# Two transformer blocks in split fp32: modulation summed on VectorE, early matmuls of ones, low halves on GpSimd

## The chip, the cores and the metric

The kernel runs on one core of a Trainium2 chip. The metric is device time in microseconds of one execution, from the first to the last instruction and what the launch adds around it; lower is better. The engines are TensorE (PE in the profile, with its weight loads as PEld), VectorE (DVE), ScalarE (ACT), GpSimd (POOL) and SyncE (SP), which issues the transfers.

## The reference, cut to what matters

Two blocks work on x of 1 x 512 tokens x 1024, all in fp32. The first runs twice (two layers):

```
h = rms_norm(x, g_pre_mix[l])
q, k, v, cb, cc, cx, ga, gb = split(h @ w_in[l])
y_attn = band_attention(rope(q), rope(k), v, sink) @ w_attn_proj[l]
y_conv = (cb * short_conv(cc * cx, conv_w[l])) @ w_conv_proj[l]
x = x + rms_norm((sigmoid(ga) * y_attn + sigmoid(gb) * y_conv) @ w_out[l], g_post_mix[l])
h = rms_norm(x, g_pre_ffn[l])
x = x + rms_norm((silu(h @ w_gate[l]) * (h @ w_up[l])) @ w_down[l], g_post_ffn[l])
```

The second block runs once. A vector c of 1024 numbers gives six vectors of 1024 that shift, scale and gate its two halves: mod = silu(c) @ ada_w + ada_b, with ada_w of 1024 x 6144. Its first half has four mixers of four heads each: stick-breaking, differential, forgetting and native sparse attention; the second half is a feed-forward part with a short convolution. Of stick-breaking attention the change touches the part that needs, for each query, running sums over keys:

```
z = q @ k.T * scale
log_beta = log_sigmoid(z)
log_keep = where(past, log_sigmoid(-z), 0)
tail = cumsum(log_keep, reverse=True) - log_keep
a = where(past, exp(log_beta + tail), 0)
o = a @ v
```

## The kernel before, in words

Activations stand with features on the partitions and the 512 tokens along the free axis. Each matmul operand is split into a high half and a low half in fp32r, and a product is three matmuls: high by high, low by high, high by low (`mm_kb`, L523 to L525, 0.227 us apart for 512 columns). `split` (L514 to L516) makes the halves of an activation: ACT casts the high half, DVE subtracts it from the source for the low one. Weights come in units of 128 x 1024: `Stream` (L255 to L268) has SP issue the transfer `raw`, ACT cast `wh` and DVE subtract `wl`, some units ahead of use. `mblock` makes one block of 128 output features by 24 matmuls. The tile scheduler of the framework sets the order on each engine from the order of the code and its own simulated times; transfers, tiles and PSUM banks come from pools, and each engine works through its own list in order.

Modulation: `ada_step` (L906 to L930) is called twice in each of 12 blocks of the gate and up products of both layers (L725 to L727 in `ffn1`), 48 units in all. A unit is 128 rows of ada_w by 1024 columns; its transfer is `adaraw` (L934). DVE multiplies it by the silu of c, one number per partition, and adds it to `adaacc` (L918 for the first of eight, L920 for the others). After eight units the sum over partitions is eight fp32 matmuls of one column against ones (L927, each two passes on PE), and DVE adds the bias from `cols` into `mod` (L930). `ada_start` forms the silu of c by small operations at the program's start.

Start: `setup` issues the first transfers; `ones`, 128 x 128, is written by DVE (L357). The first products on PE are those of `Head`, `hd`, as the halves `hh` and `hl` of x come from ACT (L447) and DVE (L448) and the weights from `Stream`.

Stick-breaking heads: `S` computes scores into three PSUM banks, forms `rz` (softplus) for each by ACT and DVE (L1462), has GpSimd zero what is not past on the diagonal (`affine_select`, L1443, two on the third bank) and splits it into `sbk` (L1466, so L515 and L516). `C`, some steps later, sums `sbk` over keys on PE (L1484). Between the heads, `pipeline` puts pieces of the next mixers' preparation. In the last mixer, `osplit` (L1331) splits six of the eight blocks of mixer output `o` into `op2h` and `op2l` as background pieces, the last two after it; GpSimd scales that mixer's probabilities `pp` (L1158).

Of the kernel before, what the change touches and what calls it, by code (L numbers as in the profile page):

```python
# [9 lines left out]
F32 = mybir.dt.float32  # L10
F32R = mybir.dt.float32r
AF = mybir.ActivationFunctionType
OP = mybir.AluOpType

P = 128
# [17 lines left out]
def col_layout():  # L33
    off, lay = 0, {}

    def add(name, n):
        nonlocal off
        lay[name] = (off, n)
        off += n

    for l in range(DEPTH):
        for n in ("g_pre_mix", "g_post_mix", "g_pre_ffn", "g_post_ffn"):
            add(f"{n}{l}", NB)
        add(f"conv_w{l}", 3 * NB)
        add(f"sink{l}", NH)
    for n, c in (("c", NB), ("ada_b", 48), ("nmg", NB), ("nfg", NB), ("fcw", 3 * NF), ("fcb", NF), ("dgq", 1),
                 ("dgk", 1), ("lam", P), ("subg", 1), ("fgq", 1), ("fgk", 1), ("fbf", 4), ("ngq", 1), ("ngk", 3),
                 ("pe", 32)):
        add(n, c)
    return lay, off  # L50
# [9 lines left out]
def fm_cols(v):  # L60
    v = np.asarray(v)
    return v.reshape(-1, P).T
# [20 lines left out]
def pack(inp):  # L83
# [43 lines left out]
    def setc(name, v):  # L127
        o, n = lay[name]
        cols[:, o:o + n] = v
# [6 lines left out]
    setc("c", fm_cols(inp["c_2"][0]))  # L136
# [39 lines left out]
    for i in range(2):  # L176
# [20 lines left out]
        "ada": np.asarray(inp["ada_w_2"])[0].reshape(NB, P, 6, U).transpose(2, 0, 1, 3).reshape(48, P, U),  # L197
# [82 lines left out]
class Kern:  # L280
# [33 lines left out]

    TAIL = 4
# [22 lines left out]
    def setup(self):  # L338
# [18 lines left out]
        nc.vector.memset(self.ones, 1.0)  # L357
        self.mhalf = self.cpool.tile([P, 4], F32, name="mhalf")
# [155 lines left out]
    def split(self, hi, lo, src):  # L514
        self.nc.scalar.copy(hi, src)  # L515
        self.nc.vector.tensor_sub(lo, src, hi.bitcast(F32))  # L516
# [378 lines left out]
    def ada_start(self):  # L895
        nc = self.nc
        self.ca = self.cpool.tile([P, NB], F32, name="ca")
        o, _ = self.lay["c"]
        c = self.cols[:, o:o + NB]
        self.sigmoid_small(self.ca, c, [P, NB])  # L900
        nc.vector.tensor_mul(self.ca, self.ca, c)
        self.mod = self.cpool.tile([P, 48], F32, name="mod")
        self.ada_i = 0
        self.ada_raw = None

    def ada_step(self):  # L906
        nc = self.nc
        i = self.ada_i
        if i >= 48:
            return  # L910
        self.ada_i += 1
        if i == 0:
            self.ada_load(0)
        t = self.ada_raw
        g, kb = divmod(i, NB)
        if kb == 0:
            self.ada_acc = self.blk("adaacc", [P, U], F32)
            nc.vector.tensor_scalar(self.ada_acc, t, self.ca[:, 0:1], None, op0=OP.mult)  # L918
        else:
            nc.vector.scalar_tensor_tensor(self.ada_acc, t, self.ca[:, kb:kb + 1], self.ada_acc, op0=OP.mult,  # L920
                                           op1=OP.add)
        if i + 1 < 48:
            self.ada_load(i + 1)
        if kb == NB - 1:
            ps = self.ps("ada")
            for m in range(NB):
                nc.tensor.matmul(ps[:, m:m + 1], self.ada_acc[:, m * P:(m + 1) * P], self.ones[:, 0:1], start=True,  # L927
                                 stop=True)
            o = self.lay["ada_b"][0] + g * NB
            nc.vector.tensor_add(self.mod[:, g * NB:(g + 1) * NB], ps[:, :NB], self.cols[:, o:o + NB])  # L930
# [261 lines left out]
    def block2(self, tail, pend):  # L1192
# [137 lines left out]
        def osplit(m):  # L1330
            self.split(op_.hi[m], op_.lo[m], o[m])  # L1331
# [101 lines left out]
    def sb_head(self, hd, Q, KH, KL, V, o):  # L1433
# [18 lines left out]
        def S():  # L1452
# [3 lines left out]
            for b in range(3):  # L1456
# [8 lines left out]
                self.split(t[:, 0, sl], t[:, 1, sl], rz[:, sl])  # L1465
# [316 lines left out]
```

## Time and profile before

| | |
|---|---|
| time, median of 3 runs | 2462.95 us (2461.41 to 2464.72) |
| profiled execution, its own time | 2465.88 us |
| its span | 2464.2 us |
| mean granted TensorE clock | 0.991 |
| busy: PE, DVE, ACT, POOL | 2407.3, 1324.1, 996.1, 399.2 us |
| chain that ended last, by engine | PE 90%, DVE 3%, ACT 3%, POOL 2% |

Busy time is the time in which an engine has an instruction under way; matmuls overlap, so the step from one start to the next is what one costs, not its duration. The chain is followed back from the last instruction to what released each one. Times in the profile count from the span's start.

### The profile page before, as it was taken

What the parts mean: (1) busy time and instruction counts of PE and PEld (TensorE: products, weight loads), DVE (VectorE), ACT (ScalarE), POOL (GpSimd) and SP (SyncE); (2) the same over time, 40 slices, a digit from 0 to 9 for tenths busy, and PEclk for the clock granted to TensorE, in tenths of its full rate; (3) what the DMA queues carried; (4) which work ended last, traced back from release to release, by engine and by line L of the source; (5) the groups of instructions that cost most, each with busy time, mean ns of one, the idle gap of its engine ahead of it and who ended that gap; (6) DMA issues with size and microseconds to landing.
All of it is one profiled execution on the core that took longest, in us unless ns stands there. A gap on an engine that the chain in (4) does not pass through costs nothing.

```text
span 2464.2 us, 32671 instructions
## 1 busy us (share of the span) xinstructions
PE 2407.3 (98%) x12680; PEld 2073.7 (84%) x12680; DVE 1324.1 (54%) x2324; ACT 996.1 (40%) x1808; POOL 399.2 (16%) x437
## 2 busy tenths in 40 slices
PE   8999999999999999999999999999898899999999
PEld 8888888888888898888888888888788878888888
DVE  6777544366533177775434655422667586644531
ACT  4555423442223245554224322322375575333420
POOL 3433001211110034230012111100021232000000
PEclk9999999999999999999999999999799999999999
DMA  4511523355423244223233553332221204233350
GB/s 159 149 61 64 165 94 103 103 196 200 149 85 121 80 144 126 69 83 99 94 98 129 181 195 137 99 107 74 91 88 53 83 22 146 78 103 103 105 171 24
DMA packets 90115, 272.77 MB, mean 111 GB/s; under 512 B 10175, under 2 KB 19007, under 8 KB 89960
## 3 DMA queue, kind: packets, MB, share of 16 engines
q1 hardware_dynamic: 89960, 270.68, 33.1%
q8 instruction: 100, 1.64, 0.3%
q14 instruction: 55, 0.45, 0.1%
HBM read 249.65 MB, written 15.22 MB: 107 GB/s over the span
## 4 chain that ended last, share of the span: by engine, by line
PE 90%; DVE 3%; ACT 3%; POOL 2%; issue 2%; DMA 0%; SPq 0%; POOLq 0%; ACTq 0%; DVEq 0%
PE ps L523 24%; PE ps L525 24%; PE ps L524 24%; PE hd L524 2%; PE hd L525 2%; PE hd L523 2%; PE o L840 2%; PE pt L815 1%; PE tm L1025 1%; PE tm L1026 1%; PE tm L1027 1%; POOL t L576 1%; POOL t L575 1%; ACT pp L378 1%; PE s L791 1%
## 5 line engine op out<-in xcount | busy, mean ns | idle before, releaser
L268 DVE TENSOR_TENSOR wl<-raw,wh 128x1024 fp32r<-128x1024 f32 x382 | 477.5, 1267 | 346.6 <-ACT wh L267 283.2
L267 ACT CAST wh<-raw 128x1024 fp32r<-128x1024 f32 x382 | 390.0, 1050 | 188.6 <-DMA raw<-in_w_dram 99.0
L525 PE MATMUL ps<-hh,wl 128*128 128x512 f32 x752 | 295.3, 393 | 0.9 <-DVE wl L268 0.8
L524 PE MATMUL ps<-hl,wh 128*128 128x512 f32 x752 | 294.9, 392 | 0.0
L523 PE MATMUL ps<-hh,wh 128*128 128x512 f32 x752 | 294.4, 392 | 0.0
L524 PE MATMUL ps<-hfl,wh 128*128 128x512 f32 x640 | 249.3, 390 | 0.0
L523 PE MATMUL ps<-hfh,wh 128*128 128x512 f32 x640 | 249.1, 390 | 0.0
L525 PE MATMUL ps<-hfh,wl 128*128 128x512 f32 x640 | 248.9, 389 | 0.0
L525 PEld LDWEIGHTS ps<-hh,wl 128*128 128x128 f32 x752 | 141.3, 188 | 29.1 <-DVE wl L268 2.1
L524 PEld LDWEIGHTS ps<-hl,wh 128*128 128x128 f32 x752 | 141.2, 188 | 27.2
L523 PEld LDWEIGHTS ps<-hh,wh 128*128 128x128 f32 x752 | 141.2, 188 | 27.1 <-ACT ot L844 0.2
L525 PE MATMUL ps<-hidh,wl 128*128 128x512 f32 (+1 forms) x396 | 145.1, 366 | 0.0
L523 PE MATMUL ps<-hidh,wh 128*128 128x512 f32 (+1 forms) x396 | 144.9, 366 | 0.0
L524 PE MATMUL ps<-hidl,wh 128*128 128x512 f32 (+1 forms) x396 | 144.7, 365 | 0.0
L378 ACT ACTIVATE pp<-pp,at_nm 128x256 f32<-128x256 f32 (+1 forms) x208 | 114.4, 553 | 68.2 <-DVE at_nm L797 60.0
L525 PEld LDWEIGHTS ps<-hfh,wl 128*128 128x128 f32 x640 | 120.1, 188 | 24.9
L524 PEld LDWEIGHTS ps<-hfl,wh 128*128 128x128 f32 x640 | 120.2, 188 | 24.7
L523 PEld LDWEIGHTS ps<-hfh,wh 128*128 128x128 f32 x640 | 120.0, 188 | 24.8
L720 POOL TENSOR_TENSOR gs<-gs,R 128x512 f32<-128x512 f32 x44 | 71.4, 1623 | 377.6 <-ACT gs L378 366.6
L524 PE MATMUL ps<-h3l,wh 128*128 128x512 f32 x320 | 124.5, 389 | 0.0
L525 PE MATMUL ps<-h3h,wl 128*128 128x512 f32 x320 | 124.5, 389 | 0.0
L523 PE MATMUL ps<-h3h,wh 128*128 128x512 f32 x320 | 124.3, 389 | 0.0
(461 smaller groups left out, 5200.3 us busy)
## 6 DMA issues: line engine op xcount, KB each, us to landing
raw<-in_w_dram SPq DMA_DIRECT2D x382, 512.0 KB, 3.7
adaraw<-in_ada_dram SPq DMA_DIRECT2D x48, 512.0 KB, 5.6
xd<-xh SPq DMA_DIRECT2D x24, 256.0 KB, 2.1
xh<-xd SPq DMA_DIRECT2D x24, 256.0 KB, 3.1
xh<-in_x_dram SPq DMA_DIRECT2D x16, 256.0 KB, 5.0
Q<-ql SPq DMA_DIRECT2D x32, 128.0 KB, 3.4
bias_d<-row_d SPq DMA_DIRECT2D x8, 320.0 KB, 7.5
KH<-kst SPq DMA_DIRECT2D x16, 128.0 KB, 3.9
```

The lines of the kernel that those rows point to most:

```text
L267: nc.scalar.copy(hi, raw)
L268: nc.vector.tensor_sub(lo, raw, hi.bitcast(F32))
L378: i = nc.scalar.activation(out, in_, func, **kw)
L523: nc.tensor.matmul(ps[:, t], w[0][:, sl], h.hi[kb][:, t], start=first, stop=False)
L524: nc.tensor.matmul(ps[:, t], w[0][:, sl], h.lo[kb][:, t], start=False, stop=False)
L525: nc.tensor.matmul(ps[:, t], w[1][:, sl], h.hi[kb][:, t], start=False, stop=last)
L575: nc.gpsimd.tensor_mul(t2, t2, S)
L576: nc.gpsimd.tensor_add(t1, t1, t2)
L720: nc.gpsimd.tensor_mul(g, g, self.R)
L791: nc.tensor.matmul(ps[:, :n], q, KL[g][:, LO[i]:HI[i]], start=False, stop=True)
L815: nc.tensor.transpose(bank[:, c0:c0 + P], pslice(h, i)[:, c:c + P], self.ident)
L840: nc.tensor.matmul(ps[:, c0:c1], V[j][:, g * P:(g + 1) * P], t[b][:, a, c0:c1], start=(a == 0 and j == 0), stop=(a == 1 and j == 2))
```

## The change

The modulation's weights are handed over transposed: a unit is now 128 of the 6144 outputs on the partitions by the 1024 inputs. c comes as one row, broadcast by a transfer to all 128 partitions into `ca`, and ACT takes its silu, once for the units of each layer. Each unit is then one DVE instruction that multiplies it by `ca` in place, sums along the row and adds the bias into one column of `mod`; the matmuls of one column, the accumulator and the additions of the bias are gone, and so are the small operations of `ada_start` and the column c of `cols`. Units are loaded ahead within a layer, not from the first layer to the second. In `setup` eleven matmuls of ones by ones, 128 x 128, follow the writing of ones; they take one PSUM tile. `split` can be given another engine for the subtraction, which is GpSimd for `sbk` (12 subtractions) and for the six blocks of `osplit` in the last mixer.

```diff
--- before.py
+++ after.py
@@ -43,7 +43,7 @@
             add(f"{n}{l}", NB)
         add(f"conv_w{l}", 3 * NB)
         add(f"sink{l}", NH)
-    for n, c in (("c", NB), ("ada_b", 48), ("nmg", NB), ("nfg", NB), ("fcw", 3 * NF), ("fcb", NF), ("dgq", 1),
+    for n, c in (("ada_b", 48), ("nmg", NB), ("nfg", NB), ("fcw", 3 * NF), ("fcb", NF), ("dgq", 1),
                  ("dgk", 1), ("lam", P), ("subg", 1), ("fgq", 1), ("fgk", 1), ("fbf", 4), ("ngq", 1), ("ngk", 3),
                  ("pe", 32)):
         add(n, c)
@@ -133,7 +133,6 @@
             setc(f"{n}{l}", fm_cols(inp[n][l]))
         setc(f"conv_w{l}", fm_cols(inp["conv_w"][l]))
         setc(f"sink{l}", np.tile(inp["attn_sink"][l][None, :], (P, 1)))
-    setc("c", fm_cols(inp["c_2"][0]))
     setc("ada_b", fm_cols(inp["ada_b_2"][0]))
     setc("nmg", fm_cols(inp["norm_mix_g_2"][0]))
     setc("nfg", fm_cols(inp["norm_ffn_g_2"][0]))
@@ -194,7 +193,8 @@
         "onehot": onehot,
         "tab": np.ascontiguousarray(tab, np.float32),
         "phi": phib.reshape(P, 32 * P),
-        "ada": np.asarray(inp["ada_w_2"])[0].reshape(NB, P, 6, U).transpose(2, 0, 1, 3).reshape(48, P, U),
+        "ada": np.ascontiguousarray(np.asarray(inp["ada_w_2"])[0].T.reshape(48, P, U)),
+        "crow": np.ascontiguousarray(np.asarray(inp["c_2"])[0].reshape(1, U)),
         "x": np.ascontiguousarray(np.asarray(inp["x"])[0].T.reshape(NB, P, T).transpose(1, 0, 2).reshape(P, NB * T)),
     }
 
@@ -312,6 +312,7 @@
     def small(self, name, shape, dt=F32, bufs=3):
         return self.smp.tile(shape, dt, name=self.n(name), tag=name, bufs=bufs)
 
+    WARM = 11
     TAIL = 4
     NHF = 4
     NH3 = 4
@@ -355,6 +356,9 @@
         self.valid = self.cst[:, 512:520]
         self.ones = self.cpool.tile([P, P], F32, name="ones")
         nc.vector.memset(self.ones, 1.0)
+        ps = self.ps("pw")
+        for i in range(self.WARM):
+            nc.tensor.matmul(ps[:, :P], self.ones, self.ones, start=True, stop=True)
         self.mhalf = self.cpool.tile([P, 4], F32, name="mhalf")
         nc.vector.memset(self.mhalf, -0.5)
         self.R = self.cpool.tile([P, T], F32, name="R")
@@ -511,9 +515,9 @@
         rs[i] = self.rstd(acc2, HV[i])
         self.nc.scalar.copy(self.R[:, t0:t1], self.bcast(rs[i], 2)[:, :256])
 
-    def split(self, hi, lo, src):
+    def split(self, hi, lo, src, eng=None):
         self.nc.scalar.copy(hi, src)
-        self.nc.vector.tensor_sub(lo, src, hi.bitcast(F32))
+        (eng or self.nc.vector).tensor_sub(lo, src, hi.bitcast(F32))
 
     def mm_kb(self, ps, w, h, kb, first, last, wk=None, hv=(0, T)):
         nc = self.nc
@@ -893,41 +897,25 @@
         return F
 
     def ada_start(self):
-        nc = self.nc
-        self.ca = self.cpool.tile([P, NB], F32, name="ca")
-        o, _ = self.lay["c"]
-        c = self.cols[:, o:o + NB]
-        self.sigmoid_small(self.ca, c, [P, NB])
-        nc.vector.tensor_mul(self.ca, self.ca, c)
         self.mod = self.cpool.tile([P, 48], F32, name="mod")
         self.ada_i = 0
-        self.ada_raw = None
 
     def ada_step(self):
-        nc = self.nc
         i = self.ada_i
         if i >= 48:
             return
         self.ada_i += 1
-        if i == 0:
-            self.ada_load(0)
+        if i % 24 == 0:
+            self.ca = self.blk("ca", [P, U], F32)
+            self.nc.sync.dma_start(self.ca, self.a["crow"].to_broadcast([P, U]))
+            self.act(self.ca, self.ca, AF.Silu)
+            self.ada_load(i)
         t = self.ada_raw
-        g, kb = divmod(i, NB)
-        if kb == 0:
-            self.ada_acc = self.blk("adaacc", [P, U], F32)
-            nc.vector.tensor_scalar(self.ada_acc, t, self.ca[:, 0:1], None, op0=OP.mult)
-        else:
-            nc.vector.scalar_tensor_tensor(self.ada_acc, t, self.ca[:, kb:kb + 1], self.ada_acc, op0=OP.mult,
-                                           op1=OP.add)
-        if i + 1 < 48:
+        if i % 24 < 23:
             self.ada_load(i + 1)
-        if kb == NB - 1:
-            ps = self.ps("ada")
-            for m in range(NB):
-                nc.tensor.matmul(ps[:, m:m + 1], self.ada_acc[:, m * P:(m + 1) * P], self.ones[:, 0:1], start=True,
-                                 stop=True)
-            o = self.lay["ada_b"][0] + g * NB
-            nc.vector.tensor_add(self.mod[:, g * NB:(g + 1) * NB], ps[:, :NB], self.cols[:, o:o + NB])
+        o = self.lay["ada_b"][0] + i
+        self.nc.vector.tensor_tensor_reduce(out=t, in0=t, in1=self.ca, scale=1.0, scalar=self.cols[:, o:o + 1],
+                                            op0=OP.mult, op1=OP.add, accum_out=self.mod[:, i:i + 1])
 
     def ada_load(self, i):
         self.ada_raw = self.blk("adaraw", [P, U], F32)
@@ -1328,7 +1316,7 @@
         cmps = self.compress(lambda: kcvc, box)
 
         def osplit(m):
-            self.split(op_.hi[m], op_.lo[m], o[m])
+            self.split(op_.hi[m], op_.lo[m], o[m], nc.gpsimd if m < 6 else None)
 
         P1 = lambda f, *a: (lambda: f(*a))
         aq, ak = (norm_group(halves(x, 8), 8, 32) for x in xa)
@@ -1462,7 +1450,7 @@
                 nc.vector.scalar_tensor_tensor(rz[:, sl], banks[b][:, sl], 0.0, rz[:, sl], op0=OP.max, op1=OP.add)
                 diag(rz, b)
                 t = self.blk("sbk", [P, 2, T], F32R)
-                self.split(t[:, 0, sl], t[:, 1, sl], rz[:, sl])
+                self.split(t[:, 0, sl], t[:, 1, sl], rz[:, sl], nc.gpsimd)
                 ks.append(t)
             box["k"] = ks
```

On ACT, at the first modulation unit of layer 0, before (`wh` are casts of weights, `gs` the silu of a gate, `hidh` the high half of the hidden layer):

```order
L378 ACTIVATE gs_4835<-gs_4835 128x512
L515 CAST hidh_814_4872<-hidf_4870 128x512
L378 ACTIVATE gs_4916<-gs_4916 128x512
L267 CAST wh_820_4885<-raw_4687 128x1024
L267 CAST wh_824_4920<-raw_4693 128x1024
L267 CAST wh_830_4961<-raw_4843 128x1024
L267 CAST wh_834_4996<-raw_4889 128x1024
L515 CAST hidh_814_4872<-hidf_4951 128x512
L378 ACTIVATE gs_4992<-gs_4992 128x512
```
and after:

```order
L519 CAST hidh_813_4873<-hidf_4871 128x512
L267 CAST wh_819_4888<-raw_4688 128x1024
L267 CAST wh_823_4923<-raw_4694 128x1024
L382 ACTIVATE ca_4877<-ca_4877 128x1024
L382 ACTIVATE gs_4919<-gs_4919 128x512
L267 CAST wh_829_4964<-raw_4844 128x1024
L519 CAST hidh_813_4873<-hidf_4954 128x512
L267 CAST wh_833_4999<-raw_4892 128x1024
L382 ACTIVATE gs_4995<-gs_4995 128x512
```
The silu of `ca` stands behind two casts of weights and ahead of a gate's silu and the next casts.

On PE, where the first group of sums over partitions stood, before (`ps` is a block of the gate or up product, `hfh` and `hfl` the halves of its input):

```order
L523 MATMUL ps_5131<-hfh_761_4473,wh_842_5039 128x512
L927 MATMUL ada_5115<-ones,adaacc_4878 128x1 x8
L524 MATMUL ps_5131<-hfl_762_4474,wh_842_5039 128x512
L525 MATMUL ps_5131<-hfh_761_4473,wl_843_5040 128x512
L523 MATMUL ps_5166<-hfh_747_4430,wh_846_5074 128x512
```
and after, in the same block:

```order
L527 MATMUL ps_5124<-hfh_760_4474,wh_841_5042 128x512
L528 MATMUL ps_5124<-hfl_761_4475,wh_841_5042 128x512
L529 MATMUL ps_5124<-hfh_760_4474,wl_842_5043 128x512
L527 MATMUL ps_5159<-hfh_746_4431,wh_845_5077 128x512
L528 MATMUL ps_5159<-hfl_747_4432,wh_845_5077 128x512
```
The last block of three products and the next follow one another, with no group between.

On POOL, the diagonal selects of the first two stick-breaking heads, before (`rz` the softplus of the scores, one tile for each of three banks; `xa` a later mixer's operand):

```order
L1443 AFFINE_SELECT rz_14753<-rz_14753 128x128
L1443 AFFINE_SELECT rz_14762<-rz_14762 128x128
L1443 AFFINE_SELECT rz_14771<-rz_14771 128x128
L1443 AFFINE_SELECT rz_14771<-rz_14771 128x256
L1443 AFFINE_SELECT rz_15034<-rz_15034 128x128
L1443 AFFINE_SELECT rz_15043<-rz_15043 128x128
L1443 AFFINE_SELECT rz_15052<-rz_15052 128x128
L1443 AFFINE_SELECT rz_15052<-rz_15052 128x256
L1062 TENSOR_TENSOR xa_14732<-xa_14732,tm_r_14950 128x512 x2
```
and after:

```order
L1431 AFFINE_SELECT rz_14694<-rz_14694 128x128
L1431 AFFINE_SELECT rz_14703<-rz_14703 128x128
L520 TENSOR_TENSOR sbk_14700<-rz_14694,sbk_14700 128x512
L520 TENSOR_TENSOR sbk_14709<-rz_14703,sbk_14709 128x384
L1431 AFFINE_SELECT rz_14712<-rz_14712 128x128
L1431 AFFINE_SELECT rz_14712<-rz_14712 128x256
L520 TENSOR_TENSOR sbk_14719<-rz_14712,sbk_14719 128x512
L1431 AFFINE_SELECT rz_14975<-rz_14975 128x128
L1431 AFFINE_SELECT rz_14984<-rz_14984 128x128
L1431 AFFINE_SELECT rz_14993<-rz_14993 128x128
L1431 AFFINE_SELECT rz_14993<-rz_14993 128x256
L1050 TENSOR_TENSOR xa_14673<-xa_14673,tm_r_14891 128x512 x2
```
The subtractions of the first head's first two banks stand ahead of the two selects of its third bank; those of the next head follow its selects and `xa`.

## Rows read from the trace of the kernel before

**Rows 1.** The page: busy time by engine, and the chain's shares by engine.
```profile
PE 2407.3 (98%) x12680; PEld 2073.7 (84%) x12680; DVE 1324.1 (54%) x2324; ACT 996.1 (40%) x1808; POOL 399.2 (16%) x437
...
PE 90%; DVE 3%; ACT 3%; POOL 2%; issue 2%; DMA 0%; SPq 0%; POOLq 0%; ACTq 0%; DVEq 0%
```

**Rows 2.** Stretches: their bounds and length, busy time by engine, granted clock, DMA share.
```profile
20.00:61.60 41.60, 41.60 (x280) 38.58 (x279) 23.85 (x40) 13.12 (x21) 18.12 (x12) 1.00 0.30 96
554.40:616.00 61.60, 61.60 (x288) 51.45 (x286) 40.66 (x41) 18.29 (x23) 8.28 (x5) 1.00 0.54 200
1727.00:1731.00 4.00, 1.64 (x8) 1.56 (x8) 0.16 (x1) 0.00 (x0) 0.69 (x1) 0.50 0.83 260
...
1786.40:2032.80 246.40, 221.48 (x1545) 200.72 (x1543) 176.16 (x510) 163.58 (x401) 58.15 (x107) 0.98 0.19 62
```

**Rows 3.** The tile ada: PE's instructions, with min, median, max in ns.
```profile
L927 PE MATMUL ada<-ones,adaacc x96: 164/250/250, 569.7 to 1519.6; 128*128 128x1 f32 x96
```

**Rows 4.** Timeline of PE at the first group: start, duration, operation.
```profile
569.26 0.39 PE L525 MATMUL ps<-hfh,wl 128*128 128x512 f32 x1
569.48 0.39 PE L523 MATMUL ps<-hfh,wh 128*128 128x512 f32 x1
569.71 1.84 PE L927 MATMUL ada<-ones,adaacc 128*128 128x1 f32 x16
571.41 0.49 PE L524 MATMUL ps<-hfl,wh 128*128 128x512 f32 x1
571.74 0.40 PE L525 MATMUL ps<-hfh,wl 128*128 128x512 f32 x1
```

**Rows 5.** Groups of DVE by shape: busy us, mean ns, idle before.
```profile
L920 DVE SCALAR_TENSOR_TENSOR adaacc<-adaraw,ca,adaacc 128x1024 f32<-128x1024 f32 x42 | 61.9, 1474 | 0.0
...
L1145 DVE CUSTOM_DVE_ANT_0 pp<-s,F 128x512 f32<-128x512 f32 x16 | 10.8, 677 | 0.0
...
L1145 DVE DVE_READ_ACCUMULATOR2_ANT at_m<- 128x1 f32 x80 | 6.3, 79 | 0.0
```

**Rows 6.** The tile adaraw: SP's issues of its loads.
```profile
L934 SPq DMA_DIRECT2D adaraw<-in_ada_dram x48: 328/385/1257, 530.8 to 1493.4; - x48
```

**Rows 7.** The tile bias_d, one row written to many partitions: its transfers.
```profile
DMA to landing us min/median/max: 3.9/5.7/9.0
```

**Rows 8.** Timeline of ACT where the modulation begins.
```profile
539.05 2.94 ACT L267 CAST wh<-raw 128x1024 fp32r<-128x1024 f32 x3
```

**Rows 9.** Timeline of PE at the start.
```profile
6.86 0.58 PE L523 MATMUL hd<-hh,wh 128*128 128x256 f32 x1 [6.86 <-ACT hh L447]
...
13.30 0.41 PE L525 MATMUL hd<-hh,wl 128*128 128x256 f32 x1
13.51 0.41 PE L523 MATMUL hd<-hh,wh 128*128 128x256 f32 x1
...
19.00 0.28 PE L525 MATMUL hd<-hh,wl 128*128 128x256 f32 x1
19.12 0.28 PE L523 MATMUL hd<-hh,wh 128*128 128x256 f32 x1
```

**Rows 10.** The tile sbk: the sums that use it, and DVE's subtractions.
```profile
L1484 PE MATMUL c<-sbk,sbm x80: 277/282/448, 1813.2 to 1885.5; 128*128 128x256 f32 x56, 128*128 128x384 f32 x16, 128*128 128x512 f32 x8
...
L516 DVE TENSOR_TENSOR sbk<-rz,sbk x12: 646/693/1527, 1792.5 to 1843.5; 128x512 fp32r<-128x512 f32 x8, 128x384 fp32r<-128x384 f32 x4
```

**Rows 11.** Groups of GpSimd by shape.
```profile
L576 POOL TENSOR_TENSOR t<-t,t 128x512 f32<-128x512 f32 x20 | 36.7, 1839 | 1.3
...
L668 POOL TENSOR_TENSOR mixin<-mixin,z 128x512 f32<-128x512 f32 x16 | 20.6, 1288 | 331.1 <-DVE mixin L667 331.1
```

**Rows 12.** Timeline of ACT at the first selects, and of GpSimd and DVE later.
```profile
1794.06 0.62 ACT L515 CAST sbk<-rz 128x512 fp32r<-128x512 f32 x1 [1.16 <-POOL rz L1443]
...
1820.05 1.06 POOL L1062 TENSOR_TENSOR xa<-xa,tm_r 128x512 f32<-128x512 f32 x1
...
1820.13 1.53 DVE L516 TENSOR_TENSOR sbk<-rz,sbk 128x512 fp32r<-128x512 f32 x1
```
## The prediction, made before the changed kernel was run

> **What bounds the kernel now.** First the busy shares and the chain of waits [rows 1]: PE works 2407.3 of 2464.2 us and 90% of the chain that ends last is PE, so an edit counts where it changes PE's instructions, its clock, or one of the few waits before it. The stretches say where such waits are [rows 2]. In the feed-forward part of layer 0, where the modulation runs, PE is busy 61.60 of 61.60 us and DVE 40.66: time taken from DVE there buys nothing, time taken from PE counts in full. The same holds right after the start (41.60 of 41.60 between 20.00 and 61.60). In the mixers of block 2, from 1786.40 to 2032.80, PE is busy 221.48 of 246.40 us, so 24.9 us of waits are there to be won, and as much can be made worse.
>
> **Part 1, the modulation.** Removed: 96 PE passes of one column against ones, in six groups of 16 [rows 3]. Their price is what they displace, not their duration. In the first group [rows 4] the product before starts at 569.48 and the next at 571.41, the one after that at 571.74: the last one before the group, 569.26 to 569.48, gives the usual step of 0.22. From 569.48 to 571.74 are two products, usually 2 x 0.227 = 0.45; they took 2.26, so a group costs 1.81 us. Six groups: 10.8 us. PE has no idle time there, and nothing else waits for the groups, as only the modulated norms of block 2 use their result. Term: **-10.8 us**, with 9.5 to 11.5 as its ends (16 x 0.1 us is 9.6 for six, the lowest reading of the steps).
>
> Added on DVE: 48 multiply-and-sum instructions of 128x1024, each with the readout of its accumulator. The trace has the operation's nearest kin at 128x512, 677 ns, and the readout at 79 ns [rows 5]. Twice 677 is 1.35 us; the 128x1024 operation with two tensors that it replaces took 1.474 on the mean [rows 5], held up at times by GpSimd. With 1.35 or 1.474 and the 0.08, 48 of them are 69 to 75 us. Removed are 42 x 1.474 = 61.9 us and six products by a column. So DVE's load grows by 7 to 13 us over two layers, where a stretch of 61.60 us alone leaves it 21 idle [rows 2]: covered, 0. If it were not, PE would show waits for low halves of weights.
>
> Added on ACT: the silu of a row broadcast to all partitions, once per layer. The order shows it behind two casts of weights, where the engine had another silu, with casts queued behind it. It waits for its transfer. The nearest transfer of one source row to many partitions took 3.9 to 9.0 us to land [rows 7], and SP issues it first of its group, ahead of the first modulation load, with no new wait in front of it on SP. Before, the first load of this group went out at 530.8 [rows 6], so a landing within 9 us is at 539.8 at the latest, while ACT's casts there began at 539.05 [rows 8] and the silu stands behind two such casts. I take 0 for PE: a cast that comes 2 us later is still ahead of its product. If that cover were gone, 1 to 2 us in each layer: +3 as the end. The weights of unit 24 are no longer loaded ahead of the second layer's group; DVE alone waits for them.
>
> **Part 2, the eleven matmuls of ones.** They start once the ones are written, early in the 6.86 us that PE waits for the first high half [rows 9], and cost nothing if they end before that: eleven fp32 matmuls are 22 passes; one of 256 columns takes 0.21 us there, from 13.30 to 13.51 [rows 9], so these take about 4.7 us. At 0.41, the duration of such a product alone, they would take 9.0 and hold up the first products by 2 to 3 us; since those then run at what pace their halves come, an end of +1 is kept. Their gain, if any, is the clock. PE steps by 0.21 us for 256 columns at 13.30, and by 0.12 from 19.00 to 19.12: the level was 1.2 GHz until about 18.9 and 2.4 after. The columns of the granted clock say 1.00 for the whole start, so here the steps decide. From 13.30 to 19.00 are 27 steps; at 0.12 each they would take 3.2 instead of 5.7 us: **2.5 us** at most, and PE is unbroken afterwards, so what is won stays won. But weights and low halves come at their own pace there, and PE had begun its products at 6.86 without a rise before 13.30. Elsewhere in the trace the clock was down where PE worked 1.64 of 4.00 us (0.50 granted from 1727 to 1731) [rows 2]. So the warm-up may lift the level and lose it again, or not lift it. I take **-1.0**, between +1 and -2.5.
>
> By the Trainium skill, "TensorE: Matmul & The Clock Gate", section "Part 1: The HAM clock gate", the low level is the default, activity releases it, and the moment differs from run to run. The steps at 13.30 and 19.00 agree with the first half; no row here shows the second. By it the full 2.5 us would be possible in some executions and nothing in others.
>
> **Part 3, low halves on GpSimd.** DVE loses 12 subtractions with a median of 693 ns [rows 10] and six more of the same shape: 18 x 0.69 = 12.4 us, more by the slow ones. GpSimd gains 18. Its nearest row, a sum of two tensors of that shape, took 1.288, the dearest 1.839 [rows 11]: 18 x 1.288 = 23 us (up to 33), on an engine with 58.15 busy of 246.40 us [rows 2]. The low half of a head is used later, when its running sums are formed on PE: from the first of DVE's subtractions at 1792.5 to the first of PE's sums at 1813.2 are 20.7 us [rows 10], so 0.6 us more for each is hidden. What PE can win are its waits for DVE; of the freed 12.4 us I give it a tenth, about -1, since most of DVE's work there has time to spare. What it can lose: the order puts two subtractions ahead of the last diagonal selects of the first head, and ACT already waited 1.16 us for such a select [rows 12]. 2 x 1.288 = 2.6 us later comes the third cast there. Taken together **-1.0**, between -5 (two fifths of the freed time) and +5 (two heads of 2.6 each).
>
> The row that speaks against this part: at 1819 to 1821 GpSimd multiplies a tensor for 1.06 us and DVE's subtraction beside it takes 1.53 [rows 12], against that median of 0.693. Each engine held the other up. If all 18 moved ones did this to a DVE instruction, 18 x 0.84 = 15.1 us come back on DVE, more than the 12.4 freed.
>
> By the Trainium skill, "SBUF — State Buffer", section "Who interferes with whom", a VectorE instruction with two inputs in SBUF and a GpSimd instruction that reads SBUF shut each other out for the whole instruction. The 1.53 agrees with it. By that rule the moved work would free nothing on DVE wherever DVE is busy with such instructions.
>
> **The sum.** -10.8 - 1.0 - 1.0 = -12.8. From the profiled execution, 2465.88 us (span 2464.2 and 1.7 around it), that gives 2453.1. That execution lay 2.9 above the median of the runs, 2462.95; against the median 2450.2, rounded **2450 us**.
>
> **Rivals.**
> A, the forecast: all of part 1, a little of the others; 2446 to 2453.5.
> B, the modulation alone: the clock rises where it did and the halves pay for themselves with contention. 2462.95 - 10.8 = 2452.2, with the low reading 2453.5. This lies inside the same range and differs by its traces only.
> C, the halves cost: GpSimd holds up selects, later scales and DVE, +5 on PE, and the warm-up gives nothing: 2462.95 - 10.8 + 5 = 2457. For it: the 1.16 and the 1.53. Against: PE waits for DVE more than for GpSimd in that stage, and the halves are needed late.
> D, slower than before: the moved subtractions stand in GpSimd's list in front of what releases PE (the diagonal selects, `xa` and the scales of the last mixer), and each is passed on whole: 18 x 1.288 = 23.2 us, 2462.95 - 10.8 + 23.2 = 2475. It turns slower when over 10.8 + 4.9 = 15.7 us, two thirds of that, reach PE. Against: GpSimd is idle three quarters of the stage.
> E, the change does not do what it says: the silu's transfer waits and holds the casts in both layers, +3 each with the halves at 0: 2462.95 - 10.8 + 6 = 2458.2, no change by measurement. Against: the order has no wait ahead of it on SP.
> F, more is won: the full 2.5 us of clock, and -5 from the halves: 2462.95 - 10.8 - 7.5 = 2444.7.
>
> **Chances and range.** A 0.47, B 0.25, C 0.10, E 0.05, F 0.08, D 0.05. The range from 2444 to 2458 takes in A, B, C and F; outside lie D and part of E. A measurement of this kernel tells about 0.2%, 4.9 us, from no change: faster is below 2458.0, slower above 2467.9. Faster: A, B, C and F, 0.90; the 0.05 of E and some edge of D are the same, 0.06; slower 0.04. The likeliest case's own range is 2446 to 2453.5.
>
> **What would show it.** Part 1: PE without the one-column groups in the feed-forward stretches, still busy 61.60 of 61.60, and DVE's new instruction at 1.27 to 1.35 us; a wait of PE for low weights there would make it wrong. The silu at ACT with no more than 2 us of idle time ahead of it. Part 2: the warm-ups ending before 6.9 and a step of 0.12 us earlier than 18.9; if the steps change at the same time as before, its term is 0. Part 3: PE's idle time between 1786 and 2033, 24.9 us before, at 23 to 25; GpSimd's subtraction near 1.3 us; more than 30 us idle there means C or D. The whole prediction is wrong if PE's idle time grows in a stretch where it had none.

## The result, and the profile after

| | before | changed |
|---|---|---|
| median, us (lowest to highest, runs) | 2463.84 (2461.41 to 2466.24, 4) | 2450.63 (2449.31 to 2453.12, 4) |
| span of the profiled execution, us | 2464.2 | 2451.4 |

The changed kernel takes 0.9948 of the time of before (95% interval 0.993 to 0.9965): 13.2 us less, where 13 were forecast, at 2450.63 against 2450.

The profile page of the changed kernel, first busy time by engine, then the chain's shares by engine (before: [rows 1]):

```profile
PE 2401.0 (98%) x12606; PEld 2067.4 (84%) x12606; DVE 1317.9 (54%) x2341; ACT 996.1 (41%) x1809; POOL 408.6 (17%) x455
...
PE 93%; DVE 3%; ACT 2%; issue 1%; POOL 1%; DMA 0%; SPq 0%; ACTq 0%; POOLq 0%; DVEq 0%
```

PE's busy time fell by 6.3 us, although the early matmuls add 5.1. Three of the stretches of [rows 2], the last one 12.4 us earlier:

```profile
20.00:61.60 41.60, 41.60 (x277) 38.43 (x276) 24.55 (x39) 13.91 (x22) 17.17 (x12) 1.00 0.31 98
554.40:616.00 61.60, 61.60 (x273) 51.02 (x273) 43.61 (x55) 18.90 (x24) 7.33 (x6) 1.00 0.61 224
1774.00:2020.40 246.40, 221.79 (x1539) 201.08 (x1538) 167.25 (x493) 162.94 (x400) 79.98 (x128) 0.97 0.19 62
```

In the stretch of the modulation PE is as full as before, now with products of the block alone: 273 matmuls in 61.60 us, where before there were 288, 28 of them of one column. In the mixers it waits 24.6 us in place of 24.9, with GpSimd at 80 us in place of 58. The timeline of PE where the first group had been ([rows 4]):

```profile
567.60 0.39 PE L528 MATMUL ps<-hfl,wh 128*128 128x512 f32 x1
567.83 0.39 PE L529 MATMUL ps<-hfh,wl 128*128 128x512 f32 x1
568.05 0.39 PE L527 MATMUL ps<-hfh,wh 128*128 128x512 f32 x1
568.28 0.39 PE L528 MATMUL ps<-hfl,wh 128*128 128x512 f32 x1
```

The step is 0.22 to 0.23 us throughout. The modulation's units on DVE, by the tile `adaraw`; then ACT's timeline at its start (before: [rows 8]):

```profile
L917 DVE CUSTOM_DVE_ANT_0 adaraw<-adaraw,ca,cols x48: 1268/1274/2318, 542.3 to 1502.0; 128x1024 f32<-128x1024 f32 x48
...
DMA to landing us min/median/max: 4.1/6.0/9.1
```

```profile
535.17 2.00 ACT L267 CAST wh<-raw 128x1024 fp32r<-128x1024 f32 x2
537.07 1.05 ACT L382 ACTIVATE ca<-ca 128x1024 f32<-128x1024 f32 x1
539.12 0.63 ACT L382 ACTIVATE gs<-gs 128x512 f32<-128x512 f32 x1 [0.99 <-DVE gs L722]
```

The new instruction takes 1.27 us where undisturbed. The silu begins in the moment in which the casts before it end: it did not wait for its transfer, and the idle 0.99 us after it is a wait for DVE's `gs`. PE has no wait at all between 527 and 616, nor between 1370 and 1560 around the second silu (at 1387.83), so neither silu cost it anything. Now PE's timeline at the start ([rows 9]):

```profile
1.12 5.06 PE L361 MATMUL pw<-ones 128*128 128x128 f32 x22 [1.12 <-DVE ones L358]
6.84 0.38 PE L527 MATMUL hd<-hh,wh 128*128 128x256 f32 x1 [0.66 <-ACT hh L451]
8.09 0.39 PE L528 MATMUL hd<-hl,wh 128*128 128x256 f32 x1 [0.87 <-DVE hl L452]
8.31 0.28 PE L529 MATMUL hd<-hh,wl 128*128 128x256 f32 x1
8.43 0.28 PE L527 MATMUL hd<-hh,wh 128*128 128x256 f32 x1
...
9.48 0.39 PE L528 MATMUL hd<-hl,wh 128*128 128x256 f32 x1 [0.38 <-DVE hl L452]
...
11.28 1.86 PE L420 MATMUL pc<-ones,acc 128*128 128x1 f32 x8 [0.17 <-DVE acc L447]
...
13.36 0.41 PE L529 MATMUL hd<-hh,wl 128*128 128x256 f32 x1
13.57 0.41 PE L527 MATMUL hd<-hh,wh 128*128 128x256 f32 x1
...
17.11 0.28 PE L529 MATMUL hd<-hh,wl 128*128 128x256 f32 x1
17.22 0.28 PE L527 MATMUL hd<-hh,wh 128*128 128x256 f32 x1
```

The early matmuls end at 6.2, before the first product, which comes at 6.84 in place of 6.86. The clock is up when its products follow one another: 0.12 us from 8.31 to 8.43. But PE waits 0.87 us before 8.09 and 0.38 before 9.48, and from 13.36 to 13.57 the step is 0.21 again. It is 0.12 for good from 17.1, where before it was from 19.0. Last, GpSimd's groups of moved subtractions, by line and shape, and the first head's on the timelines of GpSimd and of ACT (before: [rows 12]):

```profile
L520 POOL TENSOR_TENSOR sbk<-rz,sbk 128x512 fp32r<-128x512 f32 x8 | 11.3, 1416 | 1.4 <-ACT sbk L519 1.4
...
L520 POOL TENSOR_TENSOR op2l<-o,op2h 128x512 fp32r<-128x512 f32 x6 | 7.7, 1281 | 7.0 <-ACT op2h L519 7.0
...
L520 POOL TENSOR_TENSOR sbk<-rz,sbk 128x384 fp32r<-128x384 f32 x4 | 4.1, 1018 | 0.0
```

```profile
1779.85 2.28 POOL L520 TENSOR_TENSOR sbk<-rz,sbk 128x512 fp32r<-128x512 f32 x2 [0.43 <-ACT sbk L519]
1782.08 0.64 POOL L1431 TENSOR_SCALAR_AFFINE_SELECT rz<-rz 128x128 f32<-128x128 f32 x2
```

```profile
1782.75 0.62 ACT L519 CAST sbk<-rz 128x512 fp32r<-128x512 f32 x1 [2.05 <-POOL rz L1431]
```

They cost 1.28 us, as the row of `mixin` said [rows 11], or 1.42 in the heads. The two of the first head stand ahead of the third bank's selects, and ACT waits 2.05 us for these, in place of 1.16. No wait of PE's between 1774 and 1900 is for GpSimd.

### The profile page after: what moved, and what is told of

Read it like the earlier page. It is cut to its first block, busy times and chain, and to the rows that moved or that the text cites. A ratio compares the mean times of both kernels' runs of the same rounds, so it can differ in the third digit from the quotient of the medians.

```text
span 2451.4 us, 32510 instructions
## 1 busy us (share of the span) xinstructions
PE 2401.0 (98%) x12606; PEld 2067.4 (84%) x12606; DVE 1317.9 (54%) x2341; ACT 996.1 (41%) x1809; POOL 408.6 (17%) x455
## 4 chain that ended last, share of the span: by engine, by line
PE 93%; DVE 3%; ACT 2%; issue 1%; POOL 1%; DMA 0%; SPq 0%; ACTq 0%; POOLq 0%; DVEq 0%
PE ps L528 24%; PE ps L527 24%; PE ps L529 24%; PE hd L528 2%; PE hd L529 2%; PE hd L527 2%; PE o L844 2%; PE tm L1013 1%; PE pt L819 1%; PE tm L1014 1%; PE tm L1015 1%; PE s L795 1%; PE s L794 1%; PE s L1132 1%; PE o L1170 1%
## 5 line engine op out<-in xcount | busy, mean ns | idle before, releaser
L268 DVE TENSOR_TENSOR wl<-raw,wh 128x1024 fp32r<-128x1024 f32 x382 | 485.4, 1288 | 359.1 <-ACT wh L267 290.8
L724 POOL TENSOR_TENSOR gs<-gs,R 128x512 f32<-128x512 f32 x44 | 63.5, 1442 | 375.7 <-ACT gs L382 364.8
```

The source lines that it names most:

```text
L268: nc.vector.tensor_sub(lo, raw, hi.bitcast(F32))
L724: nc.gpsimd.tensor_mul(g, g, self.R)
```

## The experiments

For all of them PE's products are numbered in the order in which PE ran them, without the early matmuls and the one-column products of the modulation; each kernel has the same 12584. The table gives the time in us between two such numbers in the profiled execution, and behind the stroke for how much of it the granted clock was at 1.2 GHz (at the start this includes the time up to the first rise, which is read from the steps between products). It is one profile of each kernel, not the median run.

| kernel | to 250, start | 2450 to 2750, ahead of layer 0's modulation | 2750 to 3700, modulation, layer 0 | 6700 to 7000, ahead of layer 1's | 7000 to 7800, modulation, layer 1 | 8500 to 8750, entry of block 2 | 9000 to 9250, stick-breaking | 10000 to 10500, last mixer |
|---|---|---|---|---|---|---|---|---|
| before | 43.4 / 18.9 | 42.9 / 0 | 220.9 | 40.8 / 3.4 | 186.7 | 52.0 / 25.1 | 38.9 | 81.8 |
| changed | 42.6 / 13.6 | 44.3 / 3.4 | 215.3 | 41.3 / 3.4 | 180.7 | 51.4 / 22.4 | 39.8 | 79.8 |
| changed, again | 41.9 / 12.3 | 44.2 / 3.4 | 215.3 | 42.6 / 6.8 | 180.7 | 50.2 / 19.6 | 39.8 | 79.9 |
| modulation only | 40.9 / 11.5 | 44.4 / 3.4 | 215.3 | 39.8 / 0 | 181.1 | 50.7 / 18.7 | 38.9 | 81.4 |
| before, no one-column products | 40.4 / 11.4 | 44.4 / 3.4 | 215.3 | 39.8 / 0 | 181.1 | 50.9 / 18.7 | 38.9 | 81.2 |
| 11 early matmuls only | 42.3 / 12.8 | 44.2 / 3.4 | 220.9 | 42.3 / 6.8 | 186.7 | 48.1 / 16.0 | 39.1 | 81.5 |
| halves only | 42.7 / 17.4 | 44.3 / 3.4 | 220.9 | 41.0 / 3.4 | 186.7 | 50.4 / 19.2 | 39.7 | 80.1 |
| changed without early matmuls | 42.5 / 17.2 | 44.4 / 3.4 | 215.3 | 39.8 / 0 | 181.1 | 51.5 / 22.4 | 39.8 | 79.9 |
| changed, 20 early | 41.7 / 8.8 | 44.2 / 3.4 | 215.3 | 42.6 / 6.8 | 180.7 | 50.2 / 19.5 | 39.8 | 79.6 |
| changed, 28 early | 40.4 / 6.0 | 42.9 / 0 | 215.3 | 39.2 / 0 | 181.6 | 48.1 / 16.1 | 39.8 | 80.3 / 3.4 |
| changed, 40 early | 42.3 / 5.2 | 45.5 / 6.8 | 215.3 | 40.8 / 3.4 | 181.1 | 51.0 / 18.5 | 39.7 | 80.4 |
| changed, 12 more halves moved | 43.9 / 15.5 | 44.3 / 3.4 | 215.3 | 41.5 / 3.4 | 180.7 | 51.7 / 22.2 | 40.3 | 80.1 |
| 28 early only | 40.2 / 6.3 | 42.8 / 0 | 220.9 | 40.1 / 0 | 186.3 | 51.7 / 25.3 | 39.1 | 81.4 |
| 28 early and the modulation | 40.4 / 5.0 | 44.3 / 3.4 | 215.3 | 39.2 / 0 | 181.6 | 48.4 / 15.5 | 39.1 | 81.2 |

**The modulation alone.** The changed kernel without the early matmuls and with every low half on DVE:

```diff
-        ps = self.ps("pw")
-        for i in range(self.WARM):
-            nc.tensor.matmul(ps[:, :P], self.ones, self.ones, start=True, stop=True)
-    def split(self, hi, lo, src, eng=None):
+    def split(self, hi, lo, src):
```

> The modulation's part alone; no early matmuls, all low halves on VectorE. Theory (the gain is the displaced PE passes, six groups of 1.8 us): 10.8 to 11.5 us faster than before, seen as a shift of about 5.5 us in each of the two feed-forward parts and nowhere else; near 2452.5. Rival (the gain comes from the three parts together, the modulation only a part of it): 5 to 8 us faster.

Measured: 2452.58 us, 0.9955 of before (0.9943 to 0.9968), by the ratio 11.1 us. Each of the two stretches of modulation is 5.6 us shorter (220.9 to 215.3, 186.7 to 181.1), 1.87 a group. The theory holds.

**The one-column products alone.** The kernel before without them:

```diff
-            ps = self.ps("ada")
-            for m in range(NB):
-                nc.tensor.matmul(ps[:, m:m + 1], self.ada_acc[:, m * P:(m + 1) * P], self.ones[:, 0:1], ...)
-            nc.vector.tensor_add(self.mod[:, g * NB:(g + 1) * NB], ps[:, :NB], self.cols[:, o:o + NB])
+            nc.vector.tensor_add(self.mod[:, g * NB:(g + 1) * NB], self.ada_acc[:, :NB], self.cols[:, o:o + NB])
```

> The kernel before without the 96 one-column products; VectorE still multiplies and adds all 48 units, and the bias is added to the first columns of its accumulator instead of to their sums (so mod is not the reference's). Theory (PE's displaced passes are the whole gain of the modulation's part): 11 us faster than before, 2452 to 2453.5, as fast as the modulation alone. Rival (the other order of VectorE's work and the lost additions carry part of it): 5 to 8 us faster.

Measured: 2452.87 us, 0.9953 (0.994 to 0.9965), with the same 215.3 and 181.1 us. DVE's work of 48 units is that of before here. So the whole gain of the first part is PE's displaced steps, and what DVE does in place of them cost no time that these runs can tell. The busy times of this kernel in two stretches of modulation, and then of the modulation alone:

```profile
554.40:616.00 61.60, 61.60 (x274) 51.02 (x273) 40.55 (x43) 17.93 (x23) 10.72 (x6) 1.00 0.56 206
1416.80:1478.40 61.60, 61.60 (x274) 51.01 (x273) 38.99 (x42) 18.31 (x23) 10.43 (x6) 1.00 0.53 195
```

```profile
554.40:616.00 61.60, 61.60 (x274) 51.00 (x273) 42.87 (x54) 18.31 (x23) 8.44 (x6) 1.00 0.57 209
1416.80:1478.40 61.60, 61.60 (x273) 51.00 (x273) 39.94 (x52) 18.89 (x24) 8.43 (x6) 1.00 0.53 196
```

DVE is 2.3 and 1.0 us busier with the new instructions, at the same 61.60 of PE.

**Eleven early matmuls alone.** The kernel before, with them:

```diff
+        ps = self.ps("pw")
+        for i in range(11):
+            nc.tensor.matmul(ps[:, :P], self.ones, self.ones, start=True, stop=True)
```

> Only the eleven early matmuls are added to the kernel before. Theory: the clock rises before the first product and falls back during the one-column products, so PE is 0.8 us ahead at 20 us; in the time 0 to 1.5 us, within the measurement. Rival (the early clock is worth its bound): 2.5 us faster. Second rival (the later order, shifted by one PSUM turn, costs): 1 us or more slower, with the loss between 490 and 530.

Measured: 2462.71 us, 0.9998 (0.9989 to 1.0007): no gain that can be told from 0. In the profile PE is 1.1 us ahead at product 250 (42.3 against 43.4), and 1.3 is lost ahead of layer 0's modulation (44.2 against 42.9), where the clock fell near 495 as the second rival has it; kernels without early matmuls have that fall too (modulation only, halves only), so it is not shown to come from them. The first fall came at 9.4, before the one-column products at 11.3, not during them. **The changed kernel without them** (the same lines taken out) fits:

> The changed kernel without the eleven early matmuls and their PSUM tile. Theory: the 0.8 us at the start is lost, and the low clock near 495 us, which the changed kernel has and the kernel before has not, goes away if it came from the shift by 0.8 us; net between 0.8 slower and 0.6 faster than the changed kernel, 2450 to 2452. Rival (the early matmuls are worth 2.5): 2453.

Measured: 2451.41 us, 0.9946 (0.9933 to 0.9958), where the changed kernel has 0.9948. The low clock near 495, put down to the shift by 0.8 us, is there without the shift too, so this reason falls. The start took 40.4 to 43.4 us in the five kernels without early matmuls, as the first rise came anywhere between 11.4 and 18.9 us, and 41.9 to 43.9 in the four profiles with eleven.

**The changed kernel, a second profile.**

> The changed kernel unchanged, a second profile. Theory (where the granted clock falls changes from execution to execution): the stretches at 1.2 GHz stand elsewhere or have other lengths, and its lead over before at marks on PE differs by 1 to 2 us between the two profiles outside the feed-forward parts, while the feed-forward parts give the same. Rival (the order sets the clock): the same stretches within 1 us.

Measured: 2449.71 us in one run. The stretches at 1.2 GHz moved by more than 1 us. Granted clock (the column after POOL) in the changed kernel's first profile, then in its second:

```profile
8.00:10.00 2.00, 1.53 (x10) 1.33 (x11) 2.00 (x6) 2.00 (x6) 0.00 (x0) 1.00 1.02 417
...
14.00:16.00 2.00, 2.00 (x11) 2.00 (x11) 2.00 (x5) 2.00 (x5) 0.11 (x1) 0.50 1.06 312
16.00:18.00 2.00, 2.00 (x15) 2.00 (x15) 2.00 (x6) 2.00 (x6) 0.00 (x0) 0.75 0.86 261
...
494.00:496.00 2.00, 1.41 (x7) 1.41 (x8) 2.00 (x8) 2.00 (x6) 0.88 (x1) 0.71 0.97 356
```

```profile
8.00:10.00 2.00, 1.63 (x9) 1.42 (x10) 2.00 (x5) 2.00 (x5) 0.00 (x0) 0.72 1.00 406
...
14.00:16.00 2.00, 2.00 (x12) 2.00 (x12) 2.00 (x5) 2.00 (x6) 0.00 (x0) 0.57 0.98 273
16.00:18.00 2.00, 2.00 (x19) 2.00 (x19) 2.00 (x5) 2.00 (x6) 0.00 (x0) 1.00 0.71 272
...
494.00:496.00 2.00, 2.00 (x10) 2.00 (x11) 2.00 (x6) 2.00 (x5) 0.39 (x1) 0.50 0.87 279
```

The same program falls before 10 in one execution and not in the other (0.72 and 1.00) and is back at 2.4 GHz by 16 in one, by 18 in the other (1.00 and 0.75). The stretches of modulation are equal to 0.1 us. The theory holds (41.3 against 42.6 and 51.4 against 50.2 in the table): below 2 us, a single pair of profiles says nothing on a term that goes through the clock.

**The halves alone.** The kernel before with `split` on GpSimd for `sbk` and six blocks of `op2l`, as in the change:

```diff
+            self.split(op_.hi[m], op_.lo[m], o[m], nc.gpsimd if m < 6 else None)
+                self.split(t[:, 0, sl], t[:, 1, sl], rz[:, sl], nc.gpsimd)
```

> Only the 18 subtractions moved to GpSimd. Theory: 0 to 2 us faster, won between 1786 and 2090, no other stretch moves. Rival (contention takes it back): 0 or up to 3 us slower, with VectorE instructions beside the moved ones longer.

Measured: 2462.74 us, 0.9994 (0.9985 to 1.0002): between 3.7 faster and 0.5 slower. The table tells more: among the stick-breaking heads each kernel with moved halves takes 39.7 to 39.8 us where those without take 38.9 to 39.1, 0.8 lost, and in the last mixer 79.6 to 80.4 in place of 81.2 to 81.8, some 1.4 won. What is won there are PE's waits for DVE, 4.6 us before and 2.0 in the changed kernel: PE, the first number behind the comma, has as much work in less time. The last mixer before, then changed:

```profile
1963.40:2045.20 81.80, 74.43 (x501) 62.76 (x500) 69.02 (x262) 65.75 (x179) 31.81 (x66) 1.00 0.22 69
```

```profile
1952.90:2032.70 79.80, 74.53 (x501) 62.65 (x500) 67.86 (x255) 64.21 (x178) 37.72 (x70) 1.00 0.22 71
```

Where the 0.8 us among the heads go is open: PE is idle there for 3.7 us before and 4.2 in the changed kernel, none of it in a wait for GpSimd. The page of the kernel with the halves alone, engines and busy times:

```profile
PE 2405.3 (98%) x12680; PEld 2072.1 (84%) x12680; DVE 1314.7 (53%) x2306; ACT 995.0 (40%) x1808; POOL 415.6 (17%) x455
```

DVE is 9.4 us less busy than before [rows 1]. The 18 subtractions had taken 14.3 us of it, the longest included (10.2 for `sbk`, 4.1 for the six of `op2l`), so 4.9 came back in other instructions. GpSimd is 16.4 us busier, though the moved ones take 23.0 there; its 128x128 selects, for one, took 0.30 us in place of 0.39. PE had little use for it.

**Twelve more low halves on GpSimd**, those of the attention weights `sbt`, which PE uses soon after:

```diff
-                self.split(t[:, 0, sl], t[:, 1, sl], e[:, sl])
+                self.split(t[:, 0, sl], t[:, 1, sl], e[:, sl], nc.gpsimd)
```

> The changed kernel, and also the 12 low halves of the attention weights (sbt) of the stick-breaking heads on GpSimd, which PE uses soon after. Theory (moved halves are free only where PE uses them late): 3 to 8 us slower than the changed kernel, as PE waits for GpSimd between 1790 and 1880. Rival (freed VectorE time is what counts): 0 to 2 us faster.

Measured: 2451.62 us, 0.9955 (0.9942 to 0.9967), not told apart from the changed kernel. Neither theory holds in its size: in the stick-breaking heads this kernel takes 40.3 us in place of 39.8, half a microsecond where 3 to 8 were expected. PE's waits between 1774 and 1900, who waited for whom, total, times and longest:

```profile
PE tm L1013 <- DVE ksw L1228: 3.7, 1, 3.7
PE o L1170 <- ACT sbt L519: 2.6, 3, 1.3
...
PE o L1170 <- POOL sbt L520: 0.4, 1, 0.4
```

One wait of 0.4 us for the moved halves; the 2.6 for the high halves were there before.

**More early matmuls.** Only the count differs from the changed kernel:

```diff
-    WARM = 11
+    WARM = 28
```

> The changed kernel with 28 early matmuls instead of 11. Theory (the clock falls again because PE does too little between the warm-up and the one-column products): they run at 2.4 GHz after some 6 us and so end before 9, the products after them are held up by under 1 us, and the clock still falls before 13; time within 1 us of the changed kernel. Rival (a longer warm-up carries the clock over): no step of 0.21 us after the rise, 1.5 to 2 us ahead at 20 us, 2449.

Measured with 28: 2445.44 us (2443.25 to 2447.01), 0.9924 (0.991 to 0.9937). The rival was right, and the gain is larger than it said. The last of them overlap the first product, which starts at 9.72, and from there on PE has next to no gap and the clock no fall, in this profile near 495 neither. The granted clock and PE's busy time in the start:

```profile
8.00:10.00 2.00, 2.00 (x20) 2.00 (x19) 2.00 (x5) 2.00 (x5) 0.00 (x0) 1.00 1.00 406
10.00:12.00 2.00, 2.00 (x20) 2.00 (x18) 1.90 (x6) 2.00 (x5) 0.00 (x0) 1.00 1.06 398
...
14.00:16.00 2.00, 2.00 (x16) 1.76 (x16) 2.00 (x6) 2.00 (x6) 0.93 (x1) 1.00 1.05 319
...
494.00:496.00 2.00, 2.00 (x19) 2.00 (x18) 2.00 (x5) 2.00 (x5) 0.00 (x0) 1.00 0.80 256
```

Three microseconds of delay at the first product are made good by product 250 (40.4 us), since the halves and weights have come meanwhile and PE waits for next to none. **With 20:**

> The changed kernel with 20 early matmuls. Theory (the clock falls where PE has gaps between the warm-up and the one-column products): 20 end near 8 us, leave a gap or none, and the clock stays up: 40.4 to 41 us at the 250th product, 2445 to 2448. Rival (only a warm-up that lasts until the halves are there in number carries over): falls back as with 11, 2450 to 2451.

Measured: 2448.56 us, 0.9942 (0.9929 to 0.9955). They end at 7.9; the clock falls after 12:

```profile
6.00:10.00 4.00, 3.55 (x27) 3.02 (x25) 3.51 (x7) 3.87 (x9) 0.00 (x0) 1.00 1.04 393
10.00:14.00 4.00, 3.49 (x21) 3.09 (x20) 3.90 (x14) 4.00 (x8) 0.66 (x1) 0.78 1.04 382
14.00:18.00 4.00, 4.00 (x29) 4.00 (x29) 4.00 (x9) 4.00 (x10) 0.03 (x1) 0.80 0.92 279
```

PE waited in 6 to 10 and 10 to 14 (3.55 and 3.49 of 4.00 us), so the rival holds for the fall. But the fall lasts 3.4 us in place of the 6.8 with 11, and the time lies between what the two gave. **With 40:**

> The changed kernel with 40 early matmuls. Theory (after the rise one costs about 0.13 us of PE's time and PE is then held up): 12 more than 28 delay the products by 1.5 us and win nothing; 2446.5 to 2447.5, unless the shift alone changes where the clock falls near 495 and 1345, then up to 2450. Rival (the longer the better): under 2445.

Measured: 2451.61 us, 0.9956 (0.9943 to 0.9969). No fall at the start, but the first product comes at 12.00 and product 250 at 42.3: 1.9 later than with 28. After the rise one of them costs 0.22 us (two steps of 0.11), not 0.13. The time is above what either theory gave, 6.2 above that with 28; the two profiles are 10.0 apart, and beyond the start that lies in later stretches (45.5 against 42.9 ahead of layer 0's modulation, 51.0 against 48.1 at the entry of block 2). **28 without the rest of the change:**

> The kernel before with 28 early matmuls and nothing else. Theory (28 carry the clock over the start, where 11 did not): 40.4 us at the 250th product instead of 43.4, so 2 to 3 us faster than before, 2460.5 to 2462, from the start; the later stretches at 1.2 GHz may add 1 to 3 us either way. Rival (the gain of 28 came only together with the modulation's part): 2463 to 2465.

Measured: 2458.58 us, 0.9982 (0.9973 to 0.9991), so the gain does not need the modulation's part. It lies below the range given for the start alone, and within what the later stretches were allowed to add; the start takes 40.2 us, where 40.4 were expected. **28 and the modulation, all halves on DVE:**

> 28 early matmuls and the modulation's part, all low halves on VectorE. Theory (the halves are worth about 1 us, from 0.9 lost in the stick-breaking heads and 1.5 won in the last mixer): 1 us slower than with them, 2446 to 2447.5. Rival (they are worth nothing, or cost): 2443 to 2445.5.

Measured: 2447.26 us, 0.9936 (0.9922 to 0.995), 1.8 above the kernel with the halves, within both intervals. That fits the theory, but the two profiles don't show it: 1.4 of the 3.5 us between them lie ahead of layer 0's modulation (44.3 against 42.9), where no half was moved and the clock fell in one of them.

## Why the prediction was right, point by point

**The modulation, -10.8.** Right in mechanism and size: 11.1 by the ratio, 11.2 by the two stretches; the kernel that only loses the one-column products has the same. The step price of [rows 4] was what counted; PE was full on either side.

**Its cost on DVE, 7 to 13 us more, covered.** Covered it was; the size was too high. The new instructions and their readouts took 62.8 + 3.7 = 66.5 us, and what they replace 61.9 + 4.5 + 1.0 = 67.4: the forecast took off only the 61.9, and neither the six products by a column (4.5) nor the additions of the bias (1.0). The mean of 1.317 us was under both 1.35 and 1.474, which I had taken from a doubled row and from a row whose durations go from 1.268 to 2.327. In all, DVE is 3.1 us busier with the modulation alone (1327.2 against 1324.1). Each layer's silu was free, as argued.

**The eleven early matmuls, -1.0.** Right that they end before the first product (5.06 us, forecast 4.7) and may lose the level again; the gain can't be told from 0 (between 2.7 us won and 1.7 lost). That they were weighed against a rise at 18.9 us was the weak spot: the rise of that one execution. In four others without them it came between 11.4 and 17.4. So the sign named for this part, a step of 0.12 us before 18.9, was met and says nothing of the gain. By the Trainium skill, "TensorE: Matmul & The Clock Gate", section "Part 1: The HAM clock gate", the moment of release differs from run to run; no row before showed it, and the changed kernel's two profiles do: after the fall the level was back at 17.0 in one and at 15.7 in the other (0.75 and 1.00 from 16 to 18).

**The halves, -1.0.** Between 3.7 won and 0.5 lost by the time; by the stretches 0.8 lost and 1.4 won. What was to be won was won where it was sought, in PE's waits for DVE, but in the last mixer alone. The mechanism that I feared is in the trace (2.05 us at ACT behind two subtractions), and no wait of PE's is put down to it. On DVE 4.9 of 14.3 us came back, not 15.1; GpSimd's subtraction took 1.42 in the heads and 1.28 in the last mixer. The row of 1.53 us was read too far: GpSimd's 1.06 beside it is the shortest of its four `xa`, and the same shape takes 1.05 with `xbk`, so only DVE was held up there. By the Trainium skill, "SBUF — State Buffer", section "Who interferes with whom", such pairs shut each other out; the freed 9.4 us show that much of the moved work met no such instruction.

**The sum.** By their ratios to before the three parts alone are worth 11.1, 0.5 and 1.5 us, 13.1 in all, and the whole 12.8; forecast were 12.8. That close a match is luck: the interval of the whole goes from 8.6 to 17.2 us, and the two terms of 1.0 each can't be told from 0. So the runs show the modulation's term and don't tell rival A from B; for A speaks the 1.4 us won in the last mixer, less the 0.8 lost in the heads. What I did not see was that the term of the early matmuls had 5 us in it with another count.

**What stays open.** With 28 instead of 11, 2.2 us come from the start, and the profiles agree on it: the three with 28 take 40.2 to 40.4 us to product 250, the four with eleven 41.9 to 43.9. The medians are 5.2 apart, and where the other 3 lie is open. The two profiles in the table are 9.3 apart, as that of the changed kernel was its slowest run (2453.12) and that with 28 the second fastest of five (2443.86); beyond the start they differ where the clock did not fall with 28: 42.9 against 44.3 ahead of layer 0's modulation, 39.2 against 41.3, 48.1 against 51.4. The profiles of other kernels have the short times sometimes (before, 42.9; eleven matmuls alone, 48.1), and that of 28 and the modulation has the fall near 495 (44.3), so they change from execution to execution. But the five runs with 28 all lie below the four with 11, and the eleven runs of before with 28 gain 4.6 us. Whether a program moved by 2 us meets fewer falls, and why, these runs don't settle.

## What to carry to other kernels

Where PE is full, price a small product by the steps that it displaces, not by its columns: 16 passes of one column cost 1.8 us here, and the sum on an engine with time to spare cost nothing that could be measured. A warm-up was worth most where it lasted until products followed with next to no gap: eleven matmuls that ended at 6.2 us won nothing, 28 that held up the first product by 3 us won 4.6 us on the kernel before, and 40, which held it up by 5 in the changed kernel, won nothing over eleven. Terms that go through the clock want several profiles of each kernel before they are believed.

## What the runs showed of the hardware that was not expected

The level of 2.4 GHz, reached between 6.0 and 6.8 us (the first product, at 6.84, takes 0.38 us in place of 0.58 [rows 9]), was lost again from 10.2 to 17.0, though PE was busy for all but 0.2 us from 10 to 14. Before the fall it had been busy 2.10 of 4.00 us, and before the rise 4.00 of 4.00, as these rows of the changed kernel show; so a PE that is busy now can be at the lower level.

```profile
2.00:6.00 4.00, 4.00 (x20) 3.89 (x19) 0.00 (x0) 0.75 (x2) 0.00 (x0) 1.00 0.90 262
6.00:10.00 4.00, 2.10 (x12) 1.51 (x12) 3.59 (x7) 4.00 (x10) 0.00 (x0) 1.00 1.03 377
10.00:14.00 4.00, 3.78 (x16) 3.19 (x16) 3.75 (x14) 4.00 (x9) 0.58 (x1) 0.52 1.04 391
14.00:18.00 4.00, 4.00 (x24) 4.00 (x24) 4.00 (x9) 4.00 (x10) 0.11 (x1) 0.63 0.96 286
```

At the lower level a product of 256 columns that waits for nothing steps by 0.21 us, at the higher by 0.12, so the 6.8 us at the lower level cost some 2.9 (6.8 x 0.09 / 0.21). A matmul of ones, two passes of 128 columns, cost 0.46 us at the lower level (5.06 us for eleven, their first and last passes included) and 0.22 at the higher.
